# Keys stored by residue class, four attention blocks in flight, and one buffer for the rows of the merge

## The chip, the cores and the metric

The kernel runs on one core of one Trainium2 chip. The metric is the device time of one launch, in microseconds (us); lower is better. An attention block here is 128 queries of one pair of heads against their 128 or 256 keys.

## What is computed

One decoder layer on 2048 tokens of width 1024. After a norm and an input projection, eight heads of 64 run dilated attention beside eight heads of a gated recurrence (HGRN2). Then come an output projection, and a mixture of 32 experts with two chosen per token. The change touches the attention alone:

```python
DILATED_CONFIGS = ((128, 1), (512, 4), (2048, 16))        # window, dilation
ATTN_BLOCK = 128
...
def dilated_branch(q, k, v, slopes, window, dilation):
    """Causal dilated sliding window: query t attends keys t - j*dilation, j = 0..window/dilation."""
...
    scores = jnp.einsum('bgnqhd,bgnkhd->bgnhqk', qb, kk) / math.sqrt(Dh)
    band = (sub_dist >= 0) & (sub_dist <= n_keys)
    bias = -slopes[:, None, None] * (sub_dist * dilation).astype(jnp.float32)[None]
    scores = jnp.where(valid, scores + bias, -jnp.inf)
    lse = jax.nn.logsumexp(scores, axis=-1)
    p = jnp.exp(scores - lse[..., None])
    o = jnp.einsum('bgnhqk,bgnkhd->bgnqhd', p, vv)
...
def dilated_attention(q, k, v):
    ...                                  # the three branches, each with its lse
    w = jax.nn.softmax(jnp.stack(lses, axis=0), axis=0)
    return jnp.sum(w[..., None] * jnp.stack(outs, axis=0), axis=0)
```

## The kernel before

Heads go in four pairs. For each pair the planner is given several streams of steps: `F`, the projections (16 tiles of V, 32 parts of Q and K, 64 parts for the recurrence); `A`, the attention; `H`, the recurrence in four quads. `Runner` simulates a clock with a fixed cost for each step (1290 to 1310 ns for a projection part, 430 for a score step, 330 for a value step) and delays between dependent steps. From that it writes out one order for TensorE, the same in each execution. Within it a score step has priority over projection parts, which fill the time between. The other engines' orders come from a scheduler that goes by priority; every engine's queue is then worked in order, SyncE (SP), which issues most DMAs, too.

A pair's attention runs branch 1 (dilation 1), then 3 (dilation 16), then 2 (dilation 4), 16 blocks each. In branch 3 all 16 blocks have 128 keys; in branch 2 four have 128 and twelve 256; in branch 1 one has 128 and fifteen 256. One block passes these places:

- `scores`, line 457: four matmuls into the PSUM tile `S` (two buffers). The queries are the stationary operand (LDWEIGHTS), the keys the moving one. Both are read by `block_cols` out of tiles in the order of tokens, so with a step of 1, 4 or 16 columns of two bytes.
- VectorE adds the bias and takes the maximum (L461), writes the negative maximum into `orow` (L468); ScalarE takes the exponential (L474) and its float16 half (L476); VectorE forms the low half into `Ps` (L477).
- SP transposes `Ps` into `PT` by a DMA (L479, four buffers).
- `values` (L492, L494) multiplies `PT` with V, `LAG` = 3 blocks behind the scores. ScalarE copies half of the result (L501), VectorE adds it into `orow` (L503).
- Branches 1 and 3 store `orow` to DRAM (`od`). In branch 2 `combine` merges every two blocks with the rows of the other branches, which two DMAs load into `R` (L527, two buffers): small VectorE steps for the weights (L532 to L546), two products and a sum on GpSimd (L550, L552), the last sum on VectorE (L553), and the store to `mix` (L555).

V is projected in the order of tokens, used by branch 1 from where it was written, and stored to DRAM (`vd`); branches 3 and 2 load it from there with their stride. The bias of each branch is one constant of distances times a slope, formed by GpSimd (L444).

Of the kernel before, what the change touches and what calls it, by code (L numbers as in the profile page):

```python
# [9 lines left out]
F32 = mybir.dt.float32  # L10
F32R = mybir.dt.float32r
F16 = mybir.dt.float16
# [3 lines left out]
AF = mybir.ActivationFunctionType  # L16
OP = mybir.AluOpType
# [14 lines left out]
def shape_tables():  # L32
# [23 lines left out]
    parts['d1'] = dist(128 + tt, np.concatenate([tt, 128 + tt]), 1)  # L56

# [14 lines left out]
    parts['asg'] = np.stack([tok - tok % 16, tok % 16, 1 + 0 * tok], -1).reshape(128, 96).astype(f)  # L72
    parts['spare'] = np.stack([2048 + p, 2048 + 128 + p], 1).astype(f)
    off, cols = {}, 0
    for k, v in parts.items():
# [16 lines left out]
RW = "tile"  # L92
LAG = 3
AHEAD = 250
# [70 lines left out]
class Layer:  # L165
# [188 lines left out]
    def qk_chunk(self, D, W, which, ch, part):  # L354
# [42 lines left out]
    def v_tile(self, D, W, n):  # L397
        nc = self.nc
        wh, wl = W['v']['wh'], W['v']['wl']
        if n == 0:  # L400
            D['V', 1] = self.vp.tile([128, NT, 2, 128], F16, name="V", bufs=2)
        if n % 4 == 0:
# [7 lines left out]
        if n % 4 == 3:  # L410
            q = n // 4
            pv = D['vps'].rearrange("p n (h d) -> p n h d", h=2)
            vs = D['V', 1][:, 4 * q:4 * q + 4]
# [6 lines left out]
    def load_v(self, D, br):  # L420

        nc, vd = self.nc, D['vd']
        V = D['V', br] = self.vp.tile([128, NT, 2, 128], F16, name="V", bufs=2)
        Vf = V.rearrange("p n h c -> p n (h c)")
        dil = DIL[br]
        for n in range(NT // dil):
            src = bass.AP(tensor=vd.tensor, offset=vd.offset + n * 128 * dil * 256,
                          ap=[[dil * 256, 128], [1, dil * 256]])
            nc.sync.dma_start(Vf[:, n * dil:n * dil + dil, :].rearrange("p n c -> p (n c)"), src)


    def block_cols(self, t, br, blk, keys):

        dil = DIL[br]
        r, n = blk % dil, blk // dil
        lo = n - 1 if keys and n else n
        return t[:, r + lo * 128 * dil:r + (n + 1) * 128 * dil - dil + 1:dil]

    def bias_tile(self, D, p, br):
        nc = self.nc  # L440
        b = D['bias', br] = self.ap_.tile([128, 256], F32, name="bias", bufs=2)
        col = self.asm.tile([128, 1], F32, name="slope")
        nc.vector.tensor_scalar(col, D['f'][:, 4:5], -DIL[br] * 2.0 ** -(2 * p + 2), None, op0=OP.mult)
        nc.gpsimd.tensor_scalar(b, self.c['d1'], col, 1.0, op0=OP.mult, op1=OP.mult)  # L444

    def scores(self, D, B, br, blk):
# [7 lines left out]
        for h in range(2):  # L454
            q = self.block_cols(D['q'][h], br, blk, False)
            for x in range(2):
                nc.tensor.matmul(ps[:, h, :W], q, self.block_cols(D['k'][h][:, x], br, blk, True), start=(x == 0),  # L457
                                 stop=(x == 1))
# [382 lines left out]
    def attention_steps(self, p, D, st, A):  # L841
# [5 lines left out]
        def score(i):  # L847
            br, blk = seq[i]
            if i == 0:
                self.bias_tile(D, p, br)  # L850
            if blk == 8 and br != 2:
                self.bias_tile(D, p, {1: 3, 3: 2}[br])
            with self.tc.high_priority(offset=130):
                self.scores(D, B[i], br, blk)
# [382 lines left out]
    def route_setup(self, rb, ps):  # L1237
        nc, rp = self.nc, self.rpool
        _, off = shape_tables()
        self.load_consts(rp, off['before'][0], self.aps['cst'].shape[1], "ctr")  # L1240
        self.gf = rp.tile([128, DM], F32, name="gf")
# [707 lines left out]
```

## Time and profile before

| | us |
|---|---|
| median of 3 runs (2145.69 to 2153.36) | 2147.06 |
| the profiled execution | 2147.24 |
| its span, first to last instruction | 2145.3 |
| TensorE busy | 1942.6 |
| VectorE busy | 1461.2 |
| ScalarE busy | 1178.3 |
| GpSimd busy | 404.9 |

Input norm, projections, attention and recurrence fill the first 1080 us or so: the score matmuls run from 118.7 to 1075.0 us. The output projection, routing and the experts follow. The four pairs begin their scores at about 119, 358, 605 and 857 us. The profile gives for each group of instructions the line, the engine, the tiles, and who ended the idle time before it. A matmul's recorded duration is longer than the time until the next one starts, since matmuls are pipelined; where a group's price on TensorE is asked, the start of the next instruction is the number to read.

### The profile page before, as it was taken

The page shows a single profiled execution, that of the slowest core. Times are in us where ns is not written, and L with a number is a line of the kernel's source. Part 1 is how long each engine was busy: PE and PEld are TensorE (multiplying, and loading weights), DVE is VectorE, ACT ScalarE, POOL GpSimd, SP SyncE. Part 2 cuts the span into 40 slices and gives each one's busy share as a digit, 9 for nine tenths or more (in the row PEclk, how much of TensorE's full clock was granted, in tenths as well). Part 3 has the DMA queues.
Part 4 walks back from the last instruction along what each step waited for, and adds up shares of the span by engine and source line. Part 5 has one row for each costly group of instructions (what it writes and reads, how often), then busy time and mean ns, then how long its engine had stood idle before and what let it go on. Part 6 is the DMA issues. An engine that isn't in the chain of part 4 may idle for free. (4 is left out here: it accounts for less than half of the span.)

```text
span 2145.3 us, 39433 instructions
## 1 busy us (share of the span) xinstructions
PE 1942.6 (91%) x13777; PEld 1332.6 (62%) x13777; DVE 1461.2 (68%) x4183; ACT 1178.3 (55%) x2581; POOL 404.9 (19%) x447
## 2 busy tenths in 40 slices
PE   4999989999999999898879897999999999999981
PEld 3645675555755556454444445789999977666650
DVE  7647687768857686668886677756665765656525
ACT  7456564755556565666553343656655655554423
POOL 0101132012310123103311011112333321110110
PEclk9999989999999999999899997999999999999995
DMA  8244265634545245534579994999999999999857
GB/s 266 67 94 109 63 135 128 136 73 90 148 102 124 55 109 183 127 85 104 120 207 272 271 241 164 354 343 310 312 314 315 333 315 321 317 325 330 289 149 290
DMA packets 437998, 433.88 MB, mean 202 GB/s; under 512 B 241620, under 2 KB 324692, under 8 KB 437280
## 3 DMA queue, kind: packets, MB, share of 16 engines
q1 hardware_dynamic: 420464, 382.74, 60.0%
q0 software_dynamic: 14064, 46.46, 8.7%
q8 instruction: 109, 1.79, 0.3%
q10 hardware_dynamic: 3264, 2.10, 0.3%
q14 instruction: 97, 0.79, 0.1%
HBM read 305.82 MB, written 66.29 MB: 173 GB/s over the span
## 5 line engine op out<-in xcount | busy, mean ns | idle before, releaser
L1672 DVE TENSOR_TENSOR eL<-eraw,eH 128x1024 bf16<-128x1024 f32 x252 | 302.4, 1217 | 99.0 <-ACT eH L1665 92.0
L1665 ACT ACTIVATE eH<-eraw 128x1024 fp32r<-128x1024 f32 x252 | 258.7, 1053 | 114.9 <-PE acc L1773 48.1
L474 ACT ACTIVATE P<-S,orow,fqk 128x256 f32<-128x256 f32 (+1 forms) x384 | 195.1, 512 | 174.1 <-DVE orow L468 93.0
L588 PE MATMUL proj<-whh,x 128*128 128x512 f16 x512 | 200.6, 392 | 4.1 <-ACT hq L595 4.1
L589 PE MATMUL proj<-whl,x 128*128 128x512 f16 x512 | 199.4, 389 | 0.0
L590 PE MATMUL proj<-whh,x 128*128 128x512 f16 x512 | 199.0, 389 | 0.0
L1754 PE MATMUL acc<-xs,eH 128*128 128x352 f32 (+15 forms) x1216 | 195.1, 313 | 1.2 <-DVE xs L1731 1.2
L461 DVE CUSTOM_DVE_ANT_0 S<-S,bias 128x256 f32<-128x256 f32 (+1 forms) x384 | 141.7, 369 | 75.9 <-PE S L457 72.4
L457 PE MATMUL S<-k,qs 128*128 128x256 f16 (+1 forms) x768 | 172.5, 355 | 14.0 <-ACT P L474 10.1
L1754 PEld LDWEIGHTS acc<-xs,eH 128*128 128x128 f32 x1216 | 176.2, 190 | 4.1 <-issue 2.2
L1804 PE MATMUL acc<-hs,eD 128*128 128x176 f32 (+15 forms) x1216 | 165.1, 295 | 3.7 <-DVE ts L1779 3.7
L1804 PEld LDWEIGHTS acc<-hs,eD 128*128 128x128 f32 x1216 | 161.1, 190 | 5.1 <-DVE ts L1779 4.5
L477 DVE TENSOR_TENSOR Ps<-P,Ps 128x256 f16<-128x256 f32 (+1 forms) x192 | 119.3, 621 | 59.0 <-ACT Ps L476 58.2
L1856 POOL DMA_INDIRECT x2d<-yo,sidx x49 | 104.6, 2136 | 254.9 <-DVE yo L1831 96.0
L457 PEld LDWEIGHTS <-qs 128*128 128x128 f16 x768 | 89.2, 123 | 68.2 <-issue 18.0
L1714 POOL DMA_INDIRECT xg<-h2d,gidx x49 | 56.2, 1146 | 333.1 <-PE tr L1728 160.1
L1772 PE MATMUL acc<-eH,xs 128*128 128x512 f32 x208 | 118.4, 569 | 0.0
L1816 PE MATMUL acc<-eD,hs 128*128 128x512 f32 x208 | 97.8, 608 | 21.9 <-ACT yo L1829 12.3
L476 ACT ACTIVATE Ps<-P 128x256 f16<-128x256 f32 (+1 forms) x192 | 102.6, 534 | 4.0 <-DMA PT<-Ps 1.6
L369 PE MATMUL proj<-x,wh 128*128 128x512 f16 x256 | 97.7, 382 | 1.3 <-DVE k L380 1.3
L370 PE MATMUL proj<-x,wh 128*128 128x512 f16 x256 | 97.8, 382 | 0.0
L371 PE MATMUL proj<-x,wl 128*128 128x512 f16 x256 | 97.7, 382 | 0.0
(410 smaller groups left out, 4593.4 us busy)
## 6 DMA issues: line engine op xcount, KB each, us to landing
eraw<-in_w_up_dram SPq DMA_DIRECT2D x128, 512.0 KB, 6.3
eD<-in_w_down_dram SPq DMA_DIRECT2D x128, 512.0 KB, 6.2
eraw<-in_w_gate_dram SPq DMA_DIRECT2D x124, 512.0 KB, 7.1
wraw<-in_w_in_dram SPq DMA_DIRECT2D x41, 512.0 KB, 4.4
od<-orow SPq DMA_DIRECT2D x64, 132.0 KB, 2.2
R<-od SPq DMA_DIRECT2D x64, 132.0 KB, 2.5
xt<-in_x_dram SPq DMA_DIRECT2D x16, 512.0 KB, 4.8
wraw<-in_w_out_dram SPq DMA_DIRECT2D x16, 512.0 KB, 3.9
```

Source lines behind the costliest of these rows:

```text
L457: nc.tensor.matmul(ps[:, h, :W], q, self.block_cols(D['k'][h][:, x], br, blk, True), start=(x == 0), stop=(x == 1))
L461: nc.vector.tensor_tensor_reduce(ps[:, h, :W], ps[:, h, :W], bias[:, 256 - W:256], 1.0, -3.0e38, OP.add, OP.max, mx[:, h:h + 1])
L474: nc.scalar.activation(P[:, h], ps[:, h, :W], AF.Exp, bias=nm[:, h:h + 1], scale=f[:, h:h + 1], accum_out=orow[:, 130 + h:131 + h])
L477: nc.vector.tensor_tensor(hv[:, 1], P, hv[:, 0], op=OP.subtract)
L588: nc.tensor.matmul(ps, self.XH[n // 4][:, k, ns], W['whh'][:, k, :], start=(k == 0), stop=False)
L589: nc.tensor.matmul(ps, self.XH[n // 4][:, k, ns], W['whl'][:, k, :], start=False, stop=False)
L590: nc.tensor.matmul(ps, self.XL[n // 4][:, k, ns], W['whh'][:, k, :], start=False, stop=(k == KT - 1))
L1665: self.last_high = self.nc.scalar.activation(H, raw, AF.Copy).ins
L1672: self.last_low = self.nc.vector.tensor_sub(L, raw, H.bitcast(F32)).ins
L1754: nc.tensor.matmul(gu[:, i, 0:2 * cap], w[:, o:o + 128], xs[:, k], start=(k == 0), stop=False, skip_group_check=True)
L1772: nc.tensor.matmul(gu[:, j], xs[:, k, 0], H[:, fs], start=(k == 0), stop=False)
L1804: nc.tensor.matmul(py[:, j, 0:cap], W['w_down', f][:, o:o + 128], hs[:, f], start=(f == 0), stop=(f == 3))
```

## The change

- In each group of 512 tokens K is written by residue modulo 16: token 16a + r of the group goes to column 32r + a. The reading side of the copy out of PSUM is strided for that; the writing side is contiguous. `block_keys` then reads runs of 32 columns for branches 3 and 2, and runs of 8 for branch 1. Queries stay as they were.
- Since keys of a block now come in another order, V must too. V is written to a tile of its own (`D['V']`), stored to `vd`, and branch 1 loads it back by 16 DMAs (`load_v` with br = 1). Branch 2's four loads get a permuted row order. The tiles share the same two buffers.
- Each branch has its own table of distances, which is loaded from DRAM into the bias tile some blocks ahead (`bias_load`) and multiplied in place.
- `LAG` is 4, `PT` has five buffers, `R` has one.

```diff
-LAG = 3
+LAG = 4
...
+            src = ps[a]
+            if which == 1:
+                src = src.rearrange("p (a r) -> p r a", r=16)
+                hi, lo = (x.rearrange("p (r a) -> p r a", r=16) for x in (hi, lo))
...
-            nc.scalar.activation(hi, ps[a], AF.Copy, scale=sc)
-            nc.vector.scalar_tensor_tensor(lo, ps[a], sc, hi, op0=OP.mult, op1=OP.subtract)
+            nc.scalar.activation(hi, src, AF.Copy, scale=sc)
+            nc.vector.scalar_tensor_tensor(lo, src, sc, hi, op0=OP.mult, op1=OP.subtract)
...
+        if br == 1:
+            for n in range(4 * g, 4 * g + 4):
+                src = bass.AP(tensor=vd.tensor, offset=vd.offset + n * 128 * 256,
+                              ap=[[256, 16], [16 * 256, 8], [1, 256]])
+                nc.sync.dma_start(Vf[:, n], src)
+            return
+        rows = [[4 * 256, 4], [16 * 256, 32]] if br == 2 else [[dil * 256, 128]]
...
+    def block_keys(self, t, br, blk):
+
+        r, n = blk % DIL[br], blk // DIL[br]
+        t = t.rearrange("p (g r a) -> p g r a", g=4, r=16)
+        if br == 3:
+            return t[:, :, r]
+        if br == 2:
+            return t.rearrange("p g (q c) a -> p c g q a", c=4)[:, r, max(n - 1, 0):n + 1]
+        cols = [t[:, m // 4, :, 8 * (m % 4):8 * (m % 4) + 8] for m in (n - 1, n) if m >= 0]
...
+    def bias_load(self, br):
+        a = shape_tables()[1][f'd{br}'][0]
+        self.dist = self.ap_.tile([128, 256], F32, name="bias", bufs=2)
+        self.nc.sync.dma_start(self.dist, self.aps['cst'][:, a:a + 256])
...
-        T = self.ap_.tile([128, 8, 128], F16, name="PT", bufs=4)[:, 0:4 * nk]
+        T = self.ap_.tile([128, 8, 128], F16, name="PT", bufs=5)[:, 0:4 * nk]
...
-        R = self.ap_.tile([128, 2, 2, ROW], F32, name="R", bufs=2)
+        R = self.ap_.tile([128, 2, 2, ROW], F32, name="R", bufs=1)
...
+            if br == 1 and blk % 4 == 0:
+                self.load_v(D, 1, blk // 4)
+            if blk == 8 and (br != 2 or p < self.last_pair):
+                self.bias_load({1: 3, 3: 2, 2: 1}[br])
```

How the order of two queues changes is seen in branch 2 of the second pair. Numbers behind a name tell one buffer's use from the next. First SP's queue before, from the store of one merge to the store of the second one after it:

```order
215 L555 DMA mix_63<-orow_6043 128x2x128 [waits DMAHW1_49,DVE_49]
216 L527 DMA R_6534<-od11_67 128x264 [waits DMAHW2_49]
217 L527 DMA R_6534<-od31_69 128x264 [waits DMAHW3_49]
218 L479 DMA_TRANSPOSE PT_6289<-Ps_6283 128x8x128 [waits DMAHW4_49,DVE_49,PE_49]
219 L479 DMA_TRANSPOSE PT_6354<-Ps_6348 128x8x128 [waits DMAHW5_49,DVE_49,PE_49]
220 L555 DMA mix_63<-orow_6164 128x2x128 [waits DMAHW6_49,DVE_49]
221 L527 DMA R_6679<-od11_67 128x264 [waits DMAHW7_49,Pool_49]
222 L527 DMA R_6679<-od31_69 128x264 [waits DMAHW0_49]
```

The same stretch of SP's queue after:

```order
254 L587 DMA mix_63<-orow_6078 128x2x128 [waits DMAHW0_49,DVE_49]
255 L559 DMA R_6480<-od11_67 128x264 [waits DMAHW2_49,DMAHW3_49,DMAHW1_49,Pool_49]
256 L559 DMA R_6480<-od31_69 128x264
257 L511 DMA_TRANSPOSE PT_6427<-Ps_6421 128x8x128 [waits DVE_49,PE_49]
258 L511 DMA_TRANSPOSE PT_6467<-Ps_6461 128x8x128 [waits DMAHW4_49,DVE_49,PE_49]
259 L587 DMA mix_63<-orow_6199 128x2x128 [waits DMAHW5_49,DVE_49]
```

The pattern is the same, but before, the rows loaded after the store of merge 6043 (`R_6534`) are not those of the next merge, which has the other buffer; they belong to the second one after it (6281). After, the rows loaded behind the store of 6078 are those of the very next merge, 6199.

VectorE's queue before, around the end of merge 6164 (its last sum is row 1310):

```order
1303 L541 TENSOR_TENSOR dent_6546<-w_6540,orow_6281 128x4 [waits Activation_49]
1304 L541 TENSOR_TENSOR dent_6546<-w_6540,R_6534 128x4 [waits DVE_49] x2
1305 L542 TENSOR_TENSOR den_6545<-dent_6546 128x4 [waits DVE_49]
1306 L503 TENSOR_TENSOR orow_6164<-O_6363,otmp_6410 128x2x128 [waits Activation_49]
1307 L543 TENSOR_TENSOR den_6545<-den_6545,dent_6546 128x4 [waits DVE_49]
1308 L550 TENSOR_TENSOR orow_6164<-orow_6164,w_6419 128x2x128 [waits DVE_49]
1309 L544 RECIPROCAL den_6545<-den_6545 128x4 [waits DVE_49]
1310 L553 TENSOR_TENSOR orow_6164<-orow_6164,R_6413 128x2x128 [waits DVE_49,Pool_49]
1311 L545 TENSOR_SCALAR den_6545<-den_6545,fqk_4343 128x4 [waits DVE_49]
1312 L593 TENSOR_SCALAR hq_6244<-proj_6356,hinv_3833 128x384 [waits PE_49]
```

VectorE's queue after, from the product of merge 6078 to the second minimum of merge 6199 (L585 is the old L553, L565 the old L533, L493 the old L461):

```order
1279 L582 TENSOR_TENSOR orow_6078<-orow_6078,w_6375 128x2x128 [waits DVE_49]
1280 L585 TENSOR_TENSOR orow_6078<-orow_6078,R_6369 128x2x128 [waits DVE_49,Pool_49]
1281 L625 TENSOR_SCALAR hq_6279<-proj_6396,hinv_3831 128x384 [waits PE_49]
1282 L509 TENSOR_TENSOR Ps_6421<-P_6422,Ps_6421 128x512 [waits DMAHW6_49,Activation_49]
1283 L493 ISA S_6452,mx_6457<-S_6452,bias_5595 128x256 [waits PE_49]
1284 L493 ISA mx_6457 128x1
1285 L535 TENSOR_TENSOR orow_6199<-O_6429,otmp_6477 128x2x128 [waits Activation_49]
1286 L493 ISA S_6452,mx_6457<-S_6452,bias_5595 128x256 [waits DVE_49]
1287 L493 ISA mx_6457 128x1
1288 L500 TENSOR_TENSOR orow_6419<-mx_6457,fqk_4403 128x2 [waits DVE_49]
1289 L564 TENSOR_TENSOR mn_6483<-orow_6199,R_6480 128x4 [waits DMAHW1_49]
1290 L565 TENSOR_TENSOR mn_6483<-mn_6483,R_6480 128x4 [waits DMAHW2_49,DVE_49]
```

Before, steps of two merges (6164 and 6281) alternate. After, one merge is finished, its rows' buffer is loaded again, and the next merge begins; eight rows of other work lie between.

## Rows read from the trace of the kernel before

**Rows 1.** The page's head and TensorE's line: busy us (share of span) xinstructions.

```profile
span 2145.3 us, 39433 instructions
PE 1942.6 (91%) x13777; PEld 1332.6 (62%) x13777; DVE 1461.2 (68%) x4183; ACT 1178.3 (55%) x2581; POOL 404.9 (19%) x447
```

**Rows 2.** Stretches: length, busy us (x) of each engine, granted clock, DMA share, GB/s.

```profile
660.00:720.00 60.00, 60.00 (x372) 35.11 (x370) 42.88 (x166) 39.00 (x111) 5.73 (x6) 1.00 0.42 94
...
752.00:806.00 54.00, 51.53 (x366) 30.83 (x365) 48.84 (x194) 34.67 (x94) 14.51 (x18) 0.97 0.50 113
...
850.00:1100.00 250.00, 216.83 (x1330) 122.96 (x1328) 185.05 (x642) 150.37 (x403) 62.55 (x66) 0.94 0.52 121
```

**Rows 3.** TensorE in order of time: start, us, what; a block of branches 1, 3, 2.

```profile
394.85 0.60 PE L457 MATMUL S<-k,qs 128*128 128x256 f16 x4
395.29 0.38 PE L588 MATMUL proj<-whh,x 128*128 128x512 f16 x1
395.50 0.38 PE L589 MATMUL proj<-whl,x 128*128 128x512 f16 x1
...
433.40 1.11 PE L457 MATMUL S<-k,qs 128*128 128x128 f16 x4
434.33 0.40 PE L588 MATMUL proj<-whh,x 128*128 128x512 f16 x1
...
505.35 1.08 PE L457 MATMUL S<-k,qs 128*128 128x256 f16 x4
506.25 0.24 PE L492 MATMUL O<-V,PT 128*128 128x128 f16 x1
```

**Rows 4.** Weight loads of the scores: ns min/median/max; 365 to 405, then 425 to 460.

```profile
L457 PEld LDWEIGHTS <-qs x44: 95/98/98, 366.8 to 404.0; 128*128 128x128 f16 x44
...
L457 PEld LDWEIGHTS <-qs x32: 142/148/171, 425.8 to 455.9; 128*128 128x128 f16 x32
```

**Rows 5.** Weight loads of a value step in order of time.

```profile
431.99 0.10 PEld L492 LDWEIGHTS <-PT 128*128 128x128 f16 x1
432.02 0.10 PEld L494 LDWEIGHTS <-PT 128*128 128x128 f16 x1
```

**Rows 6.** The merge on VectorE in order of time [idle before, releaser].

```profile
524.24 0.43 DVE L553 TENSOR_TENSOR orow<-orow,R 128x256 f32<-128x256 f32 x1
...
528.30 0.16 DVE L533 TENSOR_TENSOR mn<-mn,R 128x4 f32<-128x4 f32 x1 [0.56 <-DMA R<-od]
...
569.81 0.16 DVE L546 TENSOR_TENSOR w<-w,den 128x12 f32<-128x12 f32 x1
...
572.14 0.42 DVE L553 TENSOR_TENSOR orow<-orow,R 128x256 f32<-128x256 f32 x1 [0.62 <-POOL R L552]
```

**Rows 7.** SP's issues between the first two of these.

```profile
524.69 0.38 SPq L555 DMA_DIRECT2D mix<-orow  x1
525.16 0.91 SPq L527 DMA_DIRECT2D R<-od  x2
```

**Rows 8.** The page's groups: count | busy, mean ns of one | idle before, releaser.

```profile
L474 ACT ACTIVATE P<-S,orow,fqk 128x256 f32<-128x256 f32 (+1 forms) x384 | 195.1, 512 | 174.1 <-DVE orow L468 93.0
...
L461 DVE CUSTOM_DVE_ANT_0 S<-S,bias 128x256 f32<-128x256 f32 (+1 forms) x384 | 141.7, 369 | 75.9 <-PE S L457 72.4
...
L477 DVE TENSOR_TENSOR Ps<-P,Ps 128x256 f16<-128x256 f32 (+1 forms) x192 | 119.3, 621 | 59.0 <-ACT Ps L476 58.2
```

**Rows 9.** Two other steps of VectorE in order of time.

```profile
515.69 0.61 DVE L593 TENSOR_SCALAR hq<-proj,hinv 128x384 f32<-128x384 f32 x1
...
523.26 0.42 DVE L503 TENSOR_TENSOR orow<-O,otmp 128x256 f32<-128x256 f32 x1
```

**Rows 10.** TensorE's wait for PT, 100 to 1090 us: us in total, times, longest.

```profile
PE O L492 <- DMA PT<-Ps: 3.8, 6, 1.5
```

**Rows 11.** K's copy out of PSUM, and the loads of V: ns min/median/max, starts.

```profile
L380 DVE SCALAR_TENSOR_TENSOR k<-proj,k x32: 670/688/696, 64.3 to 898.8; 64x512 f16<-64x512 f32 x32
...
L429 SPq DMA_DIRECT2D V<-vd x20: 327/440/572, 114.0 to 932.5; - x20
```

More of the change, by code (lines that the diff above doesn't have):

```diff
@@ L55, in dist @@
         return np.where(ok, d, BIG).astype(f)
-    parts['d1'] = dist(128 + tt, np.concatenate([tt, 128 + tt]), 1)
     bc = lambda a: np.broadcast_to(np.asarray(a, f), (128, len(a))).copy()
@@ L73, in shape_tables @@
     parts['spare'] = np.stack([2048 + p, 2048 + 128 + p], 1).astype(f)
+    for br, tk in ((1, 16 * (tt % 8) + tt // 8), (2, 4 * (tt % 32) + tt // 32), (3, tt)):
+        parts[f'd{br}'] = dist(128 + tt, np.concatenate([tk, 128 + tk]), 1)
     off, cols = {}, 0
@@ L400, in v_tile @@
         if n == 0:
-            D['V', 1] = self.vp.tile([128, NT, 2, 128], F16, name="V", bufs=2)
+            D['V'] = self.vp.tile([128, NT, 2, 128], F16, name="V", bufs=2)
         if n % 4 == 0:
@@ L412, in v_tile @@
             pv = D['vps'].rearrange("p n (h d) -> p n h d", h=2)
-            vs = D['V', 1][:, 4 * q:4 * q + 4]
+            vs = D['V'][:, 4 * q:4 * q + 4]
             nc.scalar.activation(vs[:, :, :, 0:64], pv, AF.Copy, scale=PSC)
@@ L418, in v_tile, with load_v @@
                                 vs.rearrange("p n h c -> p n (h c)"))
-    def load_v(self, D, br):
+    def load_v(self, D, br, g=0):
         nc, vd = self.nc, D['vd']
-        V = D['V', br] = self.vp.tile([128, NT, 2, 128], F16, name="V", bufs=2)
+        if g == 0:
+            D['V', br] = self.vp.tile([128, NT, 2, 128], F16, name="V", bufs=2)
+        V = D['V', br]
         Vf = V.rearrange("p n h c -> p n (h c)")
         dil = DIL[br]
+        if br == 1:
[5 more added lines that the diff above has]
+        rows = [[4 * 256, 4], [16 * 256, 32]] if br == 2 else [[dil * 256, 128]]
@@ L426, in load_v, with block_queries @@
         for n in range(NT // dil):
-            src = bass.AP(tensor=vd.tensor, offset=vd.offset + n * 128 * dil * 256,
-                          ap=[[dil * 256, 128], [1, dil * 256]])
+            src = bass.AP(tensor=vd.tensor, offset=vd.offset + n * 128 * dil * 256, ap=rows + [[1, dil * 256]])
             nc.sync.dma_start(Vf[:, n * dil:n * dil + dil, :].rearrange("p n c -> p (n c)"), src)
-    def block_cols(self, t, br, blk, keys):
+    def block_queries(self, t, br, blk):
         dil = DIL[br]
@@ L435, in block_cols @@
         r, n = blk % dil, blk // dil
-        lo = n - 1 if keys and n else n
-        return t[:, r + lo * 128 * dil:r + (n + 1) * 128 * dil - dil + 1:dil]
+        return t[:, r + n * 128 * dil:r + (n + 1) * 128 * dil - dil + 1:dil]
+    def block_keys(self, t, br, blk):
[6 more added lines that the diff above has]
+        cols = [t[:, m // 4, :, 8 * (m % 4):8 * (m % 4) + 8] for m in (n - 1, n) if m >= 0]
+        if len(cols) == 1:
+            return cols[0]
+        a, b = cols
+        return bass.AP(tensor=a.tensor, offset=a.offset, ap=[a.ap[0], [b.offset - a.offset, 2], *a.ap[1:]])
@@ L439, in bias_tile @@
+    def bias_load(self, br):
+        a = shape_tables()[1][f'd{br}'][0]
+        self.dist = self.ap_.tile([128, 256], F32, name="bias", bufs=2)
+        self.nc.sync.dma_start(self.dist, self.aps['cst'][:, a:a + 256])
     def bias_tile(self, D, p, br):
         nc = self.nc
-        b = D['bias', br] = self.ap_.tile([128, 256], F32, name="bias", bufs=2)
+        b = D['bias', br] = self.dist
         col = self.asm.tile([128, 1], F32, name="slope")
         nc.vector.tensor_scalar(col, D['f'][:, 4:5], -DIL[br] * 2.0 ** -(2 * p + 2), None, op0=OP.mult)
-        nc.gpsimd.tensor_scalar(b, self.c['d1'], col, 1.0, op0=OP.mult, op1=OP.mult)
+        nc.gpsimd.tensor_scalar(b, b, col, 1.0, op0=OP.mult, op1=OP.mult)
@@ L454, in scores @@
         for h in range(2):
-            q = self.block_cols(D['q'][h], br, blk, False)
+            q = self.block_queries(D['q'][h], br, blk)
             for x in range(2):
-                nc.tensor.matmul(ps[:, h, :W], q, self.block_cols(D['k'][h][:, x], br, blk, True), start=(x == 0),
+                nc.tensor.matmul(ps[:, h, :W], q, self.block_keys(D['k'][h][:, x], br, blk), start=(x == 0),
                                  stop=(x == 1))
@@ L849, in score @@
             if i == 0:
+                if p == 0:
+                    self.bias_load(1)
                 self.bias_tile(D, p, br)
-            if blk == 8 and br != 2:
-                self.bias_tile(D, p, {1: 3, 3: 2}[br])
+            if br == 1 and blk % 4 == 0:
+                self.load_v(D, 1, blk // 4)
+            if blk == 8 and (br != 2 or p < self.last_pair):
+                self.bias_load({1: 3, 3: 2, 2: 1}[br])
+                if br != 2:
+                    self.bias_tile(D, p, {1: 3, 3: 2}[br])
             with self.tc.high_priority(offset=130):
@@ L1239, in route_setup @@
         _, off = shape_tables()
-        self.load_consts(rp, off['before'][0], self.aps['cst'].shape[1], "ctr")
+        self.load_consts(rp, off['before'][0], off['d1'][0], "ctr")
         self.gf = rp.tile([128, DM], F32, name="gf")
```

## The prediction

> **What bounds the kernel now.** I read the page first, then stretches of the attention phase, then TensorE's order of time in one block of each branch, then the merge on VectorE and SP, and last the waits. TensorE is busy 1942.6 of the 2145.3 us of the span [rows 1], so the question for each edit is whether it takes work off TensorE, and whether TensorE can use the time. Branch 3 can: from 660 to 720 us TensorE is busy 60.00 of 60.00 us at full clock, VectorE 42.88 [rows 2]. Branch 2 hardly can: from 752 to 806 us, 12 blocks or 6 merges, VectorE is busy 48.84 of 54.00 us (90%), so two engines are near their end there [rows 2]. In the last pair TensorE is busy 216.83 of 250.00 us, 87% [rows 2].
>
> **Reading K (a gain).** The price of a block's four score matmuls is the time from their start to the next instruction's start [rows 3]. Branch 1, 256 contiguous keys: 395.29 - 394.85 = 0.44 us. Branch 2, 256 keys at a step of 8 bytes: 506.25 - 505.35 = 0.90. Branch 3, 128 keys at a step of 32 bytes: 434.33 - 433.40 = 0.93. So a column costs 0.43, 0.88 and 1.8 ns. Two reads out of the same 16 bytes cost 1.76 ns and one costs 1.8, so I take it that what costs is the 16-byte piece, some 1.8 ns each, and that a contiguous read (eight columns, 3.4 ns on TensorE) hides it. After the change each piece gives eight columns in all three branches (runs of 32 and of 8, which begin at multiples of 8 columns). Then branch 2 falls to 0.44 and branch 1 stays at 0.44.
>
> [...]
>
> In branch 3 the matmuls become so short (128 columns, 4 x 0.055 = 0.22 us) that the weights may take over: the queries keep their step of 32 bytes, and such a load lasts 148 ns against 98 [rows 4]. A value step's contiguous loads start 0.03 us apart [rows 5], so they overlap; 0.03 and the 50 ns more make 0.08 each, 0.32 a block. Bounds: 0.22 if hidden, 4 x 0.148 = 0.59 if they don't overlap at all. I take 0.32, since loads are seen to overlap: a gain of 0.93 - 0.32 = 0.61 us (0.34 to 0.71) a block. TensorE is full there, so it counts whole in three pairs: 48 x 0.61 = 29.3 us, and at the 87% of the last pair 16 x 0.61 x 0.87 = 8.5. Together **-37.8 us**.
>
> **Branch 2 with one R (a gain and a loss).** TensorE gives 12 x 0.46 = 5.5 us a pair (the four narrow blocks left out). But a merge's rows can now be loaded only after the merge before is done, as the two queues show in front. The trace has that path: the last sum starts at 524.24 and ends 0.43 later at 524.67, SP issues the store at 524.69 and the loads at 525.16 [rows 7], and VectorE has the second half at 528.30 after waiting for it [rows 6]: 3.63 us. In the new order a copy of 0.61, a difference of 0.62, two adds of 0.37 and a sum of 0.42 lie between [rows 8, 9], 2.4 us; so 1.2 us of waiting. The last sum must wait for GpSimd too: 569.81 to 572.14 is 2.3 us from the weights to the sum [rows 6], and the new order has one to four instructions between; I take half of it hidden, 1.1 us of waiting. Before, two merges alternated and covered both.
>
> So a merge costs VectorE 48.84 / 6 = 8.1 us of work and up to 2.3 of new waiting, 10.4; TensorE's two blocks want 54.00 / 6 - 0.92 = 8.1. VectorE falls behind by up to 2.3 us a merge, 18.4 in the 8 merges of a pair. TensorE can take part of it: a score block needs the PSUM buffer of the second one before, so it feels a lag only beyond two blocks' 8.1 us less the two adds and two exponentials, 2 x 0.37 + 2 x 0.51 = 1.8 [rows 8], which leaves 6.3. The pair then loses 18.4 - 6.3 - 5.5 = 6.6 us in full. If the new waits fall into the idle time that VectorE has already (0.9 a merge), it is 0.9 x 8 - 6.3 - 5.5 = -4.6, a gain. I take the middle, +1.0 a pair: **+4 us**, bounds -18 and +26. At the very end three merges now run in a row where one did; two more times 2.3 us, partly under the output projection: **+3** (0 to 9).
>
> **Four in flight, five PT.** A value step comes one block later, and waits less for its transpose. All TensorE waits for PT are 3.8 us [rows 10]; **-2** (0 to -3.8).
>
> **Edits at nothing.** V's reload: 16 DMAs of 0.44 us [rows 11] on SP, 7 us a pair. They are queued at the pair's boundary, ahead of the new pair's first transposes, behind V's store; the scores of the new pair wait for Q and K, which TensorE projects after V, so the loads are covered by that. If not, each microsecond delays the first value steps, which have four blocks' time. The bias tables are one load a branch, issued half a branch ahead. K's copies read PSUM with a step of 64 bytes, which no row shows: 0.69 us each on VectorE [rows 11], 32 of them, as on ScalarE. Lower bound no change (nothing in a scattered read can be faster); upper bound the factor that a step costs TensorE, 1.8 / 0.43 = 4.2, which would let two copies a chunk take 5.8 us where TensorE brings the next chunk in 24 matmuls of 0.21 [rows 3], 5.0: some 3 us a chunk with ScalarE's part ahead, 16 chunks, +50 us. I take 0: these engines run at a rate slower than TensorE's, and nothing else in the trace points to such a factor; the end stays in the chance of a loss.
>
> **The sum**, against the profiled execution of 2147.24 us (span 2145.3; the median is 2147.06, so nothing is lost between them): -37.8 + 4 + 3 - 2 = -32.8, **2114 us**.
>
> **The rivals.**
> - *Branch 2 gains too*, because the merge's waits lie in VectorE's idle time: branch 2 adds 3 x 5.5 + 0.87 x 5.5 = 21.3 instead of losing 4. 2147.2 - 37.8 - 21.3 + 3 - 2 = 2089 us. For it: VectorE's idle time and the lag that TensorE tolerates. Against it: 90% busy.
> - *The gain is given back*: the merge's waits in full, 4 x 6.6 = 26.4, make 2137 us; or the weights don't overlap (0.34 a block, 21.1 us instead of 37.8), 2131, and with some of the waits past 2137. For it: the order leaves only one instruction before the last sum in some merges.
> - *The one buffer makes a loss.* The chain of rows loaded, weights, GpSimd and last sum becomes the pace of branch 2. The trace's pieces: 3.6 until the rows are there, 2.3 from the weights to the sum, 0.4 for it, and between the minimum and the weights an interval that VectorE's other work stretches to some 6, together 12 us a merge against 8.1. Then a pair loses (12 - 8.1) x 8 - 6.3 - 5.5 = 19.4, four 78, and 2147.2 - 37.8 + 78 + 1 = 2188 us. It eats up the whole gain from 10.8 us a merge on, and makes the kernel 0.5% slower from 11.1. Against it: the new order on VectorE already carries other work in between and the lag of 6.3 us is free.
> - *K in runs isn't faster*: if the cost hung on the pieces of the access pattern and not on 16 bytes, nothing would be won: 2147 + 4 + 3 - 2 = 2152 us.
>
> **How the numbers follow.** The forecast (2100 to 2136) 0.47; branch 2 gains too 0.20; given back (2137 to 2158) 0.18; no faster reading 0.05; a loss 0.10. Half a percent, 10.7 us, is about what a measurement of this kernel can tell from no change. Faster by more: 0.47 + 0.20 = 0.67. Within it: 0.18 + 0.05 = 0.23. Slower: 0.10. The range reaches from a little under the second case, 2086, to the fourth, 2152, and leaves out the loss, the top of the third case and a little at the bottom.
>
> **What would show it.** Right: a block of branch 3 takes about 0.3 us from its first score matmul to the next instruction, of branch 2 and 1 0.44; pairs are some 9 us closer together; in branch 2 VectorE waits for `R` and for GpSimd's sum 1 to 2 us a merge, and TensorE is idle more than now. Wrong: branch 3 above 0.5 us a block (the weights), branch 1 above 0.44 (runs of 8), the copy of K above 0.7 us, or branch 2's merges more than 10.8 us apart. Should branch 2 run 8.1 us a merge with TensorE full, the second case is it.

## The result and the profile after

The changed kernel takes 2204.07 us (median; 2194.14 to 2208.13), the kernel before beside it 2150.21: a ratio of 1.0238, 95% interval 1.0216 to 1.0261. It is slower; the forecast was 2114 us, faster.

The page's head after the change (against [rows 1]): span, TensorE's and VectorE's busy time, and TensorE's granted clock in 40 slices.

```profile
span 2205.4 us, 39527 instructions
...
PE 1928.0 (87%) x13777; PEld 1333.7 (60%) x13777; DVE 1461.0 (66%) x4183; ACT 1174.5 (53%) x2581; POOL 407.4 (18%) x447
...
PEclk9998988999999898998888998899999999999995
```

TensorE is busy for 14.6 us less (1942.6 to 1928.0), and is idle for 277.4 us where it was for 202.7. Its mean granted clock fell from 0.958 to 0.932, so the busy time counts more matmuls at a lower clock. The stretches that answer to [rows 2], in branch 3, in branch 2 and in the last pair:

```profile
692.00:752.00 60.00, 52.61 (x369) 31.25 (x368) 41.50 (x161) 38.24 (x113) 5.79 (x6) 0.94 0.53 90
784.00:838.00 54.00, 47.21 (x325) 29.93 (x324) 45.05 (x173) 33.22 (x88) 15.15 (x17) 0.91 0.45 104
890.00:1140.00 250.00, 211.50 (x1330) 120.62 (x1327) 174.25 (x586) 146.33 (x392) 56.98 (x60) 0.90 0.53 118
```

In branch 3 TensorE was full (60.00 of 60.00 us at clock 1.00); now it is busy 52.61 at 0.94, and the branch is no shorter (268.8 us in the four pairs before, from its first score to that of branch 2, and 277.9 after). The reading gain itself came as sized. TensorE in order of time, one block of branch 3 and one of branch 2 (against [rows 3]):

```profile
432.98 0.41 PE L489 MATMUL S<-k,qs 128*128 128x128 f16 x4
433.22 0.22 PE L524 MATMUL O<-V,PT 128*128 128x128 f16 x1
...
521.25 0.60 PE L489 MATMUL S<-k,qs 128*128 128x256 f16 x4
521.68 0.22 PE L524 MATMUL O<-V,PT 128*128 128x128 f16 x1
```

A block of branch 3 takes 0.24 us (0.93 before, 0.32 forecast), one of branch 2 0.43 (0.90). The 768 score matmuls were 172.5 us of busy time and are 107.5. So the question is where 65 us went, and what took some 55 more.

### The profile page after: what moved, and what is told of

The parts are those of the page before. It is cut to its first block, busy times and chain, and to the rows that moved or that the text cites. A ratio compares the mean times of both kernels' runs of the same rounds, so it can differ in the third digit from the quotient of the medians.

```text
span 2205.4 us, 39527 instructions
## 1 busy us (share of the span) xinstructions
PE 1928.0 (87%) x13777; PEld 1333.7 (60%) x13777; DVE 1461.0 (66%) x4183; ACT 1174.5 (53%) x2581; POOL 407.4 (18%) x447
## 5 line engine op out<-in xcount | busy, mean ns | idle before, releaser
L620 PE MATMUL proj<-whh,x 128*128 128x512 f16 x512 | 206.0, 402 | 1.7 <-ACT hq L627 1.5
L621 PE MATMUL proj<-whl,x 128*128 128x512 f16 x512 | 205.0, 400 | 0.0
L622 PE MATMUL proj<-whh,x 128*128 128x512 f16 x512 | 204.0, 398 | 0.0
L493 DVE CUSTOM_DVE_ANT_0 S<-S,bias 128x256 f32<-128x256 f32 (+1 forms) x384 | 141.4, 369 | 62.4 <-PE S L489 58.9
L509 DVE TENSOR_TENSOR Ps<-P,Ps 128x256 f16<-128x256 f32 (+1 forms) x192 | 114.7, 597 | 74.3 <-ACT Ps L508 73.0
L489 PE MATMUL S<-k,qs 128*128 128x256 f16 (+1 forms) x768 | 107.5, 264 | 33.3 <-ACT P L506 22.4
L489 PEld LDWEIGHTS <-qs 128*128 128x128 f16 x768 | 78.1, 124 | 75.5 <-issue 38.1
L1854 PE MATMUL acc<-eD,hs 128*128 128x512 f32 x208 | 101.4, 627 | 23.9 <-ACT yo L1867 14.6
L413 PE MATMUL proj<-wh,x 128*128 128x128 f16 x512 | 96.1, 230 | 14.0 <-DVE V L421 14.0
L1066 PE MATMUL po<-x,mT 128*128 128x512 f16 x240 | 95.1, 396 | 6.2 <-DMA mT<-mh 6.2
L371 PE MATMUL proj<-x,wh 128*128 128x512 f16 x256 | 99.4, 388 | 0.8 <-DVE k L386 0.7
```

Of the source, the lines that this page charges most:

```text
L489: nc.tensor.matmul(ps[:, h, :W], q, self.block_keys(D['k'][h][:, x], br, blk), start=(x == 0), stop=(x == 1))
L493: nc.vector.tensor_tensor_reduce(ps[:, h, :W], ps[:, h, :W], bias[:, 256 - W:256], 1.0, -3.0e38, OP.add, OP.max, mx[:, h:h + 1])
L620: nc.tensor.matmul(ps, self.XH[n // 4][:, k, ns], W['whh'][:, k, :], start=(k == 0), stop=False)
L621: nc.tensor.matmul(ps, self.XH[n // 4][:, k, ns], W['whl'][:, k, :], start=False, stop=False)
L622: nc.tensor.matmul(ps, self.XL[n // 4][:, k, ns], W['whh'][:, k, :], start=False, stop=(k == KT - 1))
```

## The experiments: the three parts one by one

The change has three parts: permuted keys (P), one buffer R (R1), a fourth block in flight with a fifth PT (F). I had three theories. A: R1 makes the loss. B: F does. C: P itself does, since TensorE's saved time becomes idle time and a lower clock.

**perm_alone** is P alone:

```diff
-LAG = 4
+LAG = 3
-        T = ...tile([128, 8, 128], F16, name="PT", bufs=5)...
+        T = ...tile([128, 8, 128], F16, name="PT", bufs=4)...
-        R = ...tile([128, 2, 2, ROW], F32, name="R", bufs=1)
+        R = ...tile([128, 2, 2, ROW], F32, name="R", bufs=2)
```

> The permuted keys alone: three blocks in flight, four PT, two buffers R, as before the change. Theory A (the one buffer R makes the loss: the merges run one after the other, VectorE comes late, TensorE waits and its granted clock falls): the reading gain shows and the time is about 2115 us, 2100 to 2130, at a clock of 0.95 or more. Theory B (the fourth block in flight makes it): about 2115 us too. Theory C (the permutation itself makes it: shorter scores leave TensorE idle in stages that other engines pace, and its clock falls; V's reload adds to it): 2180 us or more, clock below 0.945.

**perm_r1** keeps `bufs=1` for R, **perm_flight_r2** keeps `LAG = 4` and five PT with two R, **flight_r1** is the kernel before with `LAG = 4`, five PT and one R.

> Permuted keys and one buffer R, but three blocks in flight and four PT. Theory A (one R): 2170 to 2210 us, nearly the whole loss. Theory B (fourth block in flight): 2115 to 2135 us. Theory C (permutation): within 0.5% of what the permutation alone takes, 2180 us or more.

> The changed kernel with two buffers R again: permuted keys, four blocks in flight, five PT. Theory A (one R): 2105 to 2130 us. Theory B (fourth block in flight): 2180 us or more. Theory C (permutation): 2180 us or more.

> The kernel before with four blocks in flight, five PT and one R, its keys as they were. Theory A (one R): TensorE's longer scores hide a part of the merges' waits, 2165 to 2210 us. Theory B (fourth block in flight): the same, 2165 to 2210 us. Theory C (permutation): 2140 to 2160 us, as before.

**r1_alone** and **lag4_alone** change one line each in the kernel before (`name="R", bufs=1`; `LAG = 4`, with four PT).

> The kernel before with one buffer R and nothing else. Theory A in its narrower form (the merges then run at some 11 us each where two buffers give 8, and the pair ends later by what TensorE can't take): 2160 to 2180 us, merges 10.5 to 12 us apart in branch 2. Rival (one R costs only with the shorter scores): 2145 to 2155 us.

> The kernel before with four blocks in flight, but still four PT and two R. Theory B in its narrower form (the fourth block by itself costs some 11 us, as with the permuted keys): 2155 to 2172 us, from longer branches 1 and 3. Rival (it costs only together with one R, where a merge begins a block later and the rows of the last merges are read in a row at a pair's end): 2143 to 2154 us.

So lag4_alone is F without its fifth PT. Measured, each against the kernel before on the same chip (ratio and 95% interval). Beside it, from TensorE's order of time in the profiled execution, the sum over the four pairs of three stages, in us: from a pair's first score to its first wide block of branch 2 (branches 1 and 3, and branch 2's first four blocks), from there to its last score, and the gap to the next pair's first score (three of them).

| kernel | median | ratio | branches 1, 3 | branch 2 | gaps |
|---|---|---|---|---|---|
| before | 2150 to 2154 | 1 | 592.4 | 235.0 | 128.8 |
| r1_alone | 2180.6 | 1.0136 (1.0103 to 1.0168) | 592.6 | 231.1 | 159.0 |
| lag4_alone | 2167.8 | 1.0065 (1.0046 to 1.0084) | 613.9 | 231.7 | 130.5 |
| flight_r1 | 2203.9 | 1.0249 (1.0222 to 1.0276) | 617.6 | 238.4 | 152.9 |
| perm_alone | 2152.0 | 0.9998 (0.9980 to 1.0016) | 594.8 | 228.1 | 135.8 |
| perm_r1 | 2169.4 | 1.0091 (1.0057 to 1.0126) | 586.0 | 231.6 | 157.6 |
| perm_flight_r2 | 2163.5 | 1.0055 (1.0031 to 1.0079) | 614.0 | 228.3 | 135.6 |
| after | 2204.1 | 1.0238 (1.0216 to 1.0261) | 613.6 | 237.6 | 150.8 |

No theory holds alone: 2152.0 and 2163.5 us lie outside all three expectations for perm_alone and perm_flight_r2. Each row set against the one that lacks only the part in question (lag4_alone standing for F without P), R1 lengthens the gaps by 15 to 30 us and F branches 1 and 3 by 19 to 28. P by itself leaves the sum of the three stages about as it was (956.2 and 958.7). In medians R1 costs 26 us alone and 17 with P, F 14 alone and 11 with P; both together 52, with P or without. Beside R1 the median with P is 11 us lower than without (2169.4 and 2180.6), but the intervals of the two ratios overlap. The 12 to 24 us by which R1 and F together cost more than the sum are not explained: in the stages branch 2 takes some of it (238.4 and 237.6). In the changed kernel's profiled execution the stages hold 45.8 of the 60.1 us that it is longer; some 10 lie behind the last score, where none of the other kernels in the table differs by more than 4, and that is not explained either.

**How R1 costs.** The merges' last sums on VectorE in pair 1 (the second; pairs count from 0) of the changed kernel, in order of time, the first, the fifth and the last three of eight:

```profile
524.45 0.42 DVE L585 TENSOR_TENSOR orow<-orow,R 128x256 f32<-128x256 f32 x1
...
572.38 0.43 DVE L585 TENSOR_TENSOR orow<-orow,R 128x256 f32<-128x256 f32 x1 [1.32 <-POOL R L584]
...
584.69 0.43 DVE L585 TENSOR_TENSOR orow<-orow,R 128x256 f32<-128x256 f32 x1 [1.88 <-POOL R L584]
...
595.28 0.43 DVE L585 TENSOR_TENSOR orow<-orow,R 128x256 f32<-128x256 f32 x1 [1.31 <-POOL hw L688]
...
606.66 0.43 DVE L585 TENSOR_TENSOR orow<-orow,R 128x256 f32<-128x256 f32 x1 [1.31 <-POOL R L584]
```

Seven steps in 82.2 us are 11.7 us a merge. The kernel before has its last sums of pair 1 from 505.07 to 572.14, 9.6 a merge ([rows 6] show two of the eight). The last sum of pair 1 begins 34.8 us after the pair's last score (571.9) instead of 17.4 (554.7); in r1_alone, where only R differs, it is 35.7 (598.02 after 562.3). That is inside the gap in which TensorE projects V, Q and K of the next pair. What VectorE does there stands behind the merges in its queue. In r1_alone, VectorE in order of time, lines left out between:

```profile
585.96 0.17 DVE L651 COPY seq<-hg 128x16 f32<-128x16 f32 x1
590.37 0.17 DVE L532 TENSOR_TENSOR mn<-orow,R 128x4 f32<-128x4 f32 x1 [4.24 <-DMA R<-od]
590.45 0.16 DVE L654 TENSOR_TENSOR hw<-seq 128x8 f32<-128x8 f32 x1
590.52 0.16 DVE L286 TENSOR_REDUCE wtot<-hg 128x1 f32<-128x4 f32 x1
...
592.75 0.68 DVE L415 SCALAR_TENSOR_TENSOR V<-proj,V 128x512 f16<-128x512 f32 x1
```

VectorE stands 4.24 us for R's rows; behind that wait stand steps of the recurrence's scan (L654, and L643 at 590.60) and V's copy out of PSUM (L415). TensorE waits for such steps three times in that gap (3.4 us for V, 1.6 and 3.9 for the scan), and from 562 to 626 its clock is 0.92, busy 55.14 of 64 us, where the kernel before had 1.00 and 49.09 of 50 in its gap. Waits of 9 us (1 before) and the slower clock, some 5 us by an estimate (0.08 of 64), account for that gap being 12.6 us longer (63.1 against 50.5).

## The experiments: where the reading gain went

P alone takes 66.5 us of score matmuls off TensorE (172.5 to 106.0), but its whole busy time falls by 37.2 (1942.6 to 1905.4) and its idle time rises by 41.8 (202.7 to 244.5): the other matmuls became 29 us slower, at a clock of 0.943 instead of 0.958, and the rest is waiting. Branch 3, which was to gain, is 263.0 us long in the four pairs instead of 268.8. The largest waits of TensorE in perm_alone, 100 to 1150 us (total, times, longest; `hg` belongs to the scan):

```profile
PE O L524 <- DMA PT<-Ps: 20.2, 9, 7.6
PE S L489 <- ACT P L506: 16.8, 12, 2.8
PE hg L723 <- DVE dS L707: 9.5, 5, 4.5
```

Before, the wait for PT was 3.8 us in all [rows 10]. What a wait for PT does is seen in branch 3 of pair 2, in stretches of 3 us (length, busy us of PE, PEld, DVE, ACT, POOL, granted clock, DMA share by the packets that begin in it, GB/s), perm_alone:

```profile
688.00:691.00 3.00, 2.59 (x18) 1.35 (x15) 2.75 (x11) 2.02 (x8) 0.00 (x0) 1.00 0.87 174
691.00:694.00 3.00, 2.15 (x13) 1.43 (x11) 1.02 (x4) 0.99 (x4) 0.00 (x0) 1.00 2.15 145
694.00:697.00 3.00, 0.00 (x0) 0.00 (x0) 0.00 (x0) 0.00 (x0) 0.00 (x0) 0.75 0.35 64
697.00:700.00 3.00, 1.96 (x11) 1.18 (x12) 1.21 (x6) 0.78 (x3) 0.00 (x0) 0.50 0.33 88
700.00:703.00 3.00, 3.00 (x13) 1.37 (x12) 1.64 (x7) 2.54 (x8) 0.00 (x0) 0.62 0.22 44
703.00:706.00 3.00, 3.00 (x29) 2.41 (x28) 2.36 (x12) 1.69 (x7) 0.00 (x0) 1.00 0.36 92
```

The compute engines stand still for a transpose (4.9 us of waiting on TensorE, to 698.04), and then TensorE's granted clock is 0.50 and 0.62 in the two stretches from 697 to 703 us. In the same branch of the kernel before, VectorE and ScalarE slacken too:

```profile
685.00:688.00 3.00, 3.00 (x17) 1.79 (x16) 1.13 (x6) 0.97 (x4) 0.00 (x0) 1.00 0.48 79
```

but TensorE, which had more to do, is busy 3.00 of 3.00 us in every stretch from 685 to 700. Its slower scores covered the others' wait there.

But the transpose itself is also later than it was. SP's issue of it in perm_alone, then that of the one at the same place in the kernel before, each behind a load of raw weights:

```profile
687.39 0.38 SPq L279 DMA_DIRECT2D wraw<-in_w_in_dram  x1
688.00 4.61 SPq L511 DMA_TRANSPOSE PT<-Ps  x1
...
680.17 0.38 SPq L277 DMA_DIRECT2D wraw<-in_w_in_dram  x1
680.78 1.20 SPq L479 DMA_TRANSPOSE PT<-Ps  x1
```

Before, it had landed 5.5 us after its issue began (686.27); in perm_alone TensorE is released 10.0 us after.

**perm_noreload** and **perm_spread_v** ask for the part of V's loads. The first, as a diff; the second calls `load_v` for branches 3 and 2 with one quarter at blocks 0, 3, 6 and 9 of the branch before.

```diff
+        if br == 1:
+            D['V', 1] = D['V']
+            return
-            for n in range(4 * g, 4 * g + 4):
-                src = ...  # V reloaded in the order of the keys
```

> The permutation alone (three blocks in flight, four PT, two R), with the reload of V for branch 1 left out: branch 1's value steps read V as projected, so the rows of its keys and values no longer belong together and the sums differ. Theory D (the reload, 64 DMAs of some 0.5 to 0.6 us on SP at the pairs' boundaries, eats the reading gain): 2115 to 2130 us. Theory E (TensorE's saved time turns into waits for transposed probabilities, for ScalarE's and VectorE's steps, and into a lower granted clock in the stretches after those waits): 2142 to 2155 us, with TensorE's busy time 35 us under that of before and its idle time as much above.

> The permutation alone with V's loads for branches 3 and 2 issued in four pieces of 256 KB, one every three blocks, in place of 1 MB at once. Under theory E the stop of 4.9 us around 693 us, in which all engines wait for a transpose issued behind 1 MB of V and 0.5 MB of weights, goes: TensorE's waits for PT fall from 20 to under 10 us, the granted clock rises to 0.95, and the time is 2125 to 2142 us. If the waits for transposes are the blocks' own latency and not the queue: 2145 to 2155 us, with the waits for PT at 15 us or more.

perm_noreload: 2141.9 us, 0.9946 (0.9920 to 0.9971): the reload costs 10 us, in the gaps (129.4 against 135.8) and beyond. perm_spread_v: 2152.2, 0.9992 (0.9973 to 1.0012): no difference to perm_alone, waits for PT 22.3 us, and the same stop (4.90 us, ending at 690.64). But the edit did not spread that branch's loads. In its trace SP issues branch 2's four loads of V in pair 2 at 671.94, 672.57, 676.24 and 676.83 us, 18.7 to 13.8 us ahead of the stop's end, and perm_alone's stand just as far ahead (679.36 to 684.21, and 698.04). So this run says nothing on whether V's burst makes that transpose late.

**Branch 2's load of V.** The traces' DMA packets say more. P gives this load a new order of rows (`rows` in the diff: 4 steps of 32 rows in place of 128 rows at one step). A pair's load is 512 packets of 2 KB. In the four kernels without P they pass in 4.3 to 6.7 us, 11 to 13 at once in the mean; in the kernels with P in 11.2 to 15.7 us, 3 to 4 at once. In perm_alone the four loads end at 205.8, 441.6, 694.9 and 948.3 us, and TensorE's four longest waits for PT end at 206.9, 444.3, 698.0 and 949.7 (7.6, 4.7, 4.9 and 1.5 us, 18.7 of the 20.2). In each kernel with P at least 9.5 us of such waits end within 5 us behind these loads; without P none do. So P's own load is very likely what makes those transposes late. No run has P with that load in its old order, so the cause is not shown by a change, and its price isn't measured.

**perm_order_p** keeps V as projected and puts branch 1's probabilities in its order as they are split; three variants of it issue the raw weights' loads by `nc.gpsimd.dma_start` (perm_p_wpool) or `nc.scalar.dma_start` (perm_p_wact) in place of `nc.sync`, or set `name="Ps", bufs=3` (perm_p_ps3).

```diff
+        if br == 1:
+            src = P.rearrange("p h (m r a) -> p (h m) r a", r=16, a=8) ...
+            hi, lo = (halves.rearrange("p (x g a r) -> p x g r a", x=2, a=8, r=16)[:, x] for x in range(2))
+        nc.scalar.activation(hi, src, AF.Copy)
+        nc.vector.tensor_tensor(lo, src, hi, op=OP.subtract)
```

> The permutation alone with branch 1's probabilities put back into the order of V when ScalarE and VectorE split them into halves (both write 16-bit columns at a step of 32 bytes there), so that V needs no reload. If such writes cost ScalarE and VectorE nothing, as the copies of K out of PSUM did (0.69 us before and after): 2138 to 2146 us, the time of the kernel without the reload. If they cost a factor (0.41 us a cast or a difference becoming 0.8 or more): 2150 us or more.

> As perm_order_p, with the loads of raw weights (0.5 MB each) issued by GpSimd on its own queue in place of SP's. Theory G (in branch 3 the transposes stand in SP's queue behind weights and rows, and TensorE's stops of 4 to 7 us there come from that): TensorE's waits for PT fall from 20 to under 8 us and the time to 2115 to 2132 us. Rival (the transposes are late because the DMA engines themselves are full, or since the block's chain over VectorE and ScalarE is late): waits for PT stay above 14 us, time 2136 to 2150 us.

> As perm_order_p, with the loads of raw weights issued by ScalarE. Theory G: waits for PT under 8 us, as with GpSimd, but ScalarE then waits where it issues (for the buffer that VectorE's split frees), so 2118 to 2145 us. Rival: waits for PT above 14 us, 2136 to 2155 us.

> As perm_order_p, with three buffers Ps for the halves that the transposes read. In the stops of branch 3 ScalarE waits 5.4 us for a transpose to free Ps, and VectorE behind it. If that wait makes the next blocks late too: 2125 to 2138 us. If the transposes in flight are what is late, and a third buffer only lets more of them queue: 2137 to 2148 us, waits for PT as before at 15 to 20 us.

perm_order_p: 2334.4 us, 1.0859 (1.0815 to 1.0904). The split's groups, all branches together (108 wide ones, 60 of them in branch 1):

```profile
L509 DVE TENSOR_TENSOR Ps<-P,Ps 128x512 f16<-128x512 f32 x108 | 177.6, 1644 | 133.8 <-ACT Ps L508 133.6
L508 ACT ACTIVATE Ps<-P 128x512 f16<-128x512 f32 x108 | 172.5, 1597 | 1.6
```

ScalarE's mean is 1597 ns where it was 629; one in branch 1 takes 2.37 us (172.5 us less the 48 others at 0.629, over 60). The variants: weights issued by GpSimd 2359.6 us (1.0964, 1.0911 to 1.1018) with 40.1 us of waits for PT; by ScalarE 2362.3 (1.0976, 1.0936 to 1.1015) with 31.7; a third Ps 2330.1 (1.0816, 1.0778 to 1.0855) with 29.5; without any of them 29.4. So moving the weights out of SP's queue makes the waits no shorter, in a kernel that is itself slower. All four have branch 2's slow load of V.

**perm_read_s** does the reordering on the reading side instead: the exponential reads the scores in PSUM in V's order.

```diff
+            dst, src = P[:, h], ps[:, h, :W]
+            if br == 1:
+                dst = dst.rearrange("p (m a r) -> p m a r", a=8, r=16)
+                src = src.rearrange("p (m r a) -> p m a r", r=16, a=8)
+            nc.scalar.activation(dst, src, AF.Exp, ...)
```

> The permutation alone, with branch 1's probabilities brought into the order of V by the exponential, which reads the scores in PSUM at a step of 32 bytes and writes P in a row, so that V needs no reload and the casts write in a row. If the reading side is free on ScalarE, as in the copies of K (steps of 64 bytes in PSUM, 0.69 us before and after): the exponential stays at 0.56 us and the time is 2136 to 2146 us, 0.3 to 0.7% under the kernel before. If it costs like the 16-bit writes at a step of 32 bytes (2.37 against 0.63 us): 2300 us or more.

> As perm_read_s with three buffers Ps. If ScalarE's wait for Ps (5 us at the stop of each pair's branch 3) makes the blocks behind it late too: 2125 to 2137 us. If only the transposes in flight are late: as perm_read_s within 0.3%.

> As perm_read_s with three buffers R, the other side of the change's one. One R made a merge take some 12 us where two give 9.4, and cost 17 to 26 us. If the rows' loads still hold merges up with two buffers: merges under 9 us apart, 5 us or more faster than perm_read_s. If two cover the loads, as I expect: within 0.3% of perm_read_s.

perm_read_s: 2144.1 us, 0.9967 (0.9953 to 0.9981), 0.3% under the kernel before; the wide exponential takes 558 ns where it took 559. With a third Ps 2141.3, 0.9956 (0.9940 to 0.9972), the lowest median here, though not clear of perm_read_s; with three R 2144.0, 0.9968 (0.9947 to 0.9988). So two R cover the rows' loads, and ScalarE's wait for Ps is worth little.

**perm_read_s_again** puts work without use back on TensorE:

```diff
+            for _ in range({1: 0, 2: 2, 3: 3}[br]):
+                nc.tensor.matmul(ps[:, h, :W], q, self.block_keys(D['k'][h][:, 0], br, blk), start=True, stop=True)
```

> As perm_read_s, with work put back on TensorE that has no use: the first score matmul of each half is issued again, three times more in branch 3 and twice more in branch 2 (640 matmuls of 128 or 256 columns, by the 0.06 and 0.11 us of one some 24 to 38 us in branch 3 and 25 in branch 2, about what the permutation took away). If the reading time saved is worth nothing, since the attention stages end by other engines' chains, its return costs nothing: 2138 to 2152 us, TensorE busier by 40 us or more and idle for as much less. If TensorE's work sets the time and the gain went elsewhere: 2180 us or more.

2166.2 us, 1.0070 (1.0050 to 1.0090): 22 us more than perm_read_s, between the two expectations. A block of branch 3 in it, on TensorE in order of time:

```profile
431.52 0.34 PE L485 MATMUL S<-k,qs 128*128 128x128 f16 x3
431.70 0.29 PE L487 MATMUL S<-k,qs 128*128 128x128 f16 x2
431.82 0.35 PE L485 MATMUL S<-k,qs 128*128 128x128 f16 x3
432.01 0.29 PE L487 MATMUL S<-k,qs 128*128 128x128 f16 x2
432.13 0.38 PE L622 MATMUL proj<-whh,x 128*128 128x512 f16 x1
```

0.61 us against 0.24; branch 2's wide blocks take 0.87 (523.49 to 524.36) against 0.43. That is 64 x 0.37 + 48 x 0.44, and some 4 for the narrow ones of branch 2, 49 us. But TensorE's busy time rose by 17.3 (1905.8 to 1923.1) and its idle time stayed (236.5 and 236.3): the clock went from 0.943 to 0.958. If what the mean clock falls short of 1 is counted as work not done, this gives back 0.057 x 2142 - 0.042 x 2159 = 31 us, an estimate from the clocks and spans of the two runs, and 49 - 31 = 18 fits the 17.3. By that estimate about two thirds of the 49 us put on come back by the clock. Work taken off is lost in the same way in part: of perm_alone's 66.5 us, 29 came back as slower matmuls. Not explained by this: it is slower than the kernel before, which reads 17 us longer still. Something else that P brings costs at least the 14 us between them. Branch 2's load of V is one candidate (waits for PT 12.3 us against 3.8). The bias tables, now loaded three times a pair ahead of GpSimd's products, are a weaker one: GpSimd waits 43.1 us for them in six places, but after four of these it soon stands idle again for 7 us or more. Neither was tried.

## The experiments: the fourth block

**perm_lag4_orow6** is perm_alone with `LAG = 4` and six row buffers; **perm_read_s_lag2** is perm_read_s_ps3 with `LAG = 2`.

> The permutation alone with four blocks in flight, four PT, two R, and six buffers for the blocks' rows in place of four. Theory H (the fourth block costs because a row buffer, held from a block's scores until its rows are stored, comes free a block later, so that VectorE waits with the maximum): 2146 to 2156 us, as the permutation alone. Rival (it costs by the order of TensorE's work: value steps a block later leave less work ahead of the steps of the other branch of the layer that wait for ScalarE and VectorE): 2158 to 2172 us, as with four blocks in flight and four row buffers.

> As perm_read_s_ps3, with two blocks in flight. If the fourth block costs by the order in which TensorE meets the other steps, more blocks in flight being the worse: 2125 to 2140 us. If three is where the transposes are just covered: TensorE's waits for PT rise from 20 us to over 60, and the time to 2165 us or more.

perm_lag4_orow6: 2162.2 us, 1.0078 (1.0050 to 1.0106), branches 1 and 3 606.9: the row buffers don't make the loss. perm_read_s_lag2: 2221.6, 1.0344 (1.0307 to 1.0381), waits for PT 47.8 us (over 60 expected); fewer than three is worse too. The waits in lag4_alone (100 to 1150 us) show which grew:

```profile
PE hg L691 <- DVE dS L675: 17.7, 5, 7.1
PE S L457 <- ACT P L474: 14.6, 11, 3.0
PE hg L636 <- ACT hq L622: 8.7, 4, 3.1
PE hg L712 <- DVE Am L703: 6.8, 2, 5.2
```

Before they were 6.7, 10.1, 5.2 and 3.7, and the one for PT, which the fourth block is to shorten, was 3.8. So it could win 3.8 us (0.5 is left) and lost more at the steps of the scan. With P it had more to win, and did shorten that wait, from 20.2 us to 14.4 in perm_flight_r2, but the kernel still lost 11. That the loss comes from the order (value steps one block later, less work ahead of those steps) is argued, not shown. TensorE's idle time rose by 8.5 us and its busy time by 13.7, at a clock of 0.950 instead of 0.958.

## Why the prediction was wrong

- **The price of a read: right.** Branch 3 0.24 us a block (0.32 forecast), branch 2 0.43, branch 1 0.44 as before. The 16-byte piece, an estimate from the 0.88 and 1.8 ns a column before, fits, and no run has a step of 16 bytes; the copy of K stayed at 0.69 us, so its upper end of +50 was empty.
- **"TensorE is full there, so it counts whole": the first step that failed.** -37.8 was forecast for branch 3 alone; in perm_alone it is 5.8 us shorter, and the kernel gained 0 from all of P, 66 us of reading. A full engine at clock 1.00 shows that it is the last to finish, not by how much. The kernel before had a pause of VectorE and ScalarE at 685 us under TensorE's work; with less of that work and a later transpose it became a stop of all. I had looked for the next engine by its busy share (42.88 of 60), where a single late transfer was next. The clock was then lower (0.50 and 0.62 in the 6 us behind the stop of 4.9), and I had priced no idle time by the clock at all: 29 us of slower matmuls in perm_alone.
- **Branch 2's load of V had no term in the sum.** Its new order of rows stood in the diff. It takes 11 to 16 us where it took 4 to 7, and TensorE's long waits for PT end right behind it; what that cost was not measured.
- **"V's reload at nothing": wrong by 10 us** (perm_noreload). The cover I named, the projection of Q and K, is the gap, and that grew by 7 us.
- **One R: +4 and +3 forecast, 17 to 26 measured.** The rival "the one buffer makes a loss" had the chain and nearly the pace (12 us a merge, 11.7 measured, past the 10.8 named as a sign of being wrong), but its price of 78 us was far off, as was the forecast's 10.4 us a merge. Both put the loss into branch 2, where VectorE is 90% busy. Branch 2 did not get longer (231.1 us against 235.0); the late merges ran into the gap, where V's copy and the scan's steps stand behind them. The step that failed is the pair's account, 18.4 - 6.3 - 5.5: it let TensorE make up the lag inside the pair, and asked nowhere what the last merges are queued ahead of.
- **Four in flight: -2 forecast, +11 to +14 measured.** I counted only the wait that it shortens. The move of every value step by one block against the scan's steps was in the order of instructions, and I gave it no cost.
- **The chances.** 0.10 on a loss counted one mechanism. R1 and F each lose by one of their own, and P, which was to pay for them, won nothing.

## What to carry to other kernels

An engine that is busy all the time is worth speeding up only by the slack of the next chain (perm_alone took 66.5 us of score matmuls off TensorE and gained 0); look for stretches where the other engines already stand still, because those are what its work covers. On TensorE a wait was paid twice here, once as idle time and once as slower matmuls after it (in perm_alone 41.8 us more of idle time, and 29 us at a mean clock of 0.943 instead of 0.958). When data is stored in a new order, look at every transfer that follows that order, and in the trace at whether an edit moved what it was meant to move. When buffers are cut, look at the end of the phase: what stands behind the late work in the same queue pays (in r1_alone V's copy, behind VectorE's 4.24 us for R), not the stretch where the buffer is used.

## What the runs showed of the hardware

- Writing 16-bit columns to SBUF at a step of 32 bytes took ScalarE 2.37 us for a cast of 512 columns that takes 0.63 in a row; VectorE's 108 differences of that size, 60 of them at that step, took 1.64 us in the mean where they take 0.74. Reading PSUM at a step cost ScalarE nothing: 32 bytes in the exponential (558 and 559 ns), 64 bytes in K's copy (0.59 us before and after), on VectorE too (0.69 us before and after). No run here has TensorE at such a step in PSUM; the reads above, by ScalarE and VectorE, had no two neighbours together and were not slowed.
- After 4.9 us without work TensorE had a granted clock of 0.50 and 0.62 in the two stretches of 3 us from 697 us on (perm_alone), and with some 49 us of useless matmuls its mean clock was 0.958 instead of 0.943 (perm_read_s_again against perm_read_s).
- Branch 2's load of V, 1 MB in four DMAs from SP, took 11.2 to 15.7 us with 3 to 4 packets at once where its rows go in 4 steps of 32, and 4.3 to 6.7 us with 11 to 13 at once where 128 rows go in one step.
